# Decoder trunk with top-2 experts: sending expert outputs back to their tokens by row transfers in place of one-hot products, for seven of eight experts

## The chip, the cores and the metric

One core of a Trainium2 chip runs the whole program. The metric is the device time of one execution in microseconds (us). Times here are read either from repeated executions (the median of three) or from one profiled execution, of which the profiler kept a trace of every engine: PE is TensorE (matrix products), PEld its weight loads, DVE is VectorE, ACT is ScalarE, POOL is GpSimd, SP is SyncE, which issues most of the transfers.

## The reference

Two layers over 256 tokens of width 1024, in float32. Layer 0 mixes tokens with an mLSTM and then runs a dense feed-forward block; layer 1 mixes with an S5 recurrence and then runs the experts. Each half ends in a residual and a layer norm. The change touches the expert half of layer 1 alone:

```python
def moe_ffn(u, w_router, w13, w2):          # 8 experts, D = 1024, D_FF = 2816
    t = u.reshape(-1, D)
    logits = (t @ w_router).astype(jnp.float32)
    top_val, top_idx = lax.top_k(logits, TOP_K)      # TOP_K = 2
    top_w = jax.nn.softmax(top_val, axis=-1)
    out = jnp.zeros_like(t)
    for e in range(N_EXPERTS):
        gate_e = jnp.sum(jnp.where(top_idx == e, top_w, 0.0), axis=-1).astype(t.dtype)
        out = out + gate_e[:, None] * swiglu(t, w13[e], w2[e])
    return out.reshape(Bsz, S, D)
...
x = layer_norm(DEEPNORM_ALPHA * x + (1.0 + g_f) * y, ln_ffn_g[i], ln_ffn_b[i])
```

A token has two experts, so an expert needs to see about a quarter of the tokens.

## The kernel before, in words

The expert half is `experts` (called by `moe`). Its outer loop `e` runs over eight *places*; the router sorts the experts into them, so that the fuller ones come into even places. An even place has room for 96 tokens (`SA + SB` = 64 + 32 slots), an odd place for 64. If an expert overflows, a branch behind the loop runs a second pass; the loop itself does not depend on it.

Into a place: `gather` multiplies the tokens with one-hot matrices (token by slot), so that `xs[e]` holds the tokens of its slots, in columns.

Within a place, six blocks `b` of the hidden width:

- `first(e, b)` fetches four pieces of `moe_w13` (two in block 5) with `tile` (line 1424, on SP) and multiplies them with the tokens into `eg` and, in even places, `eu` (lines 1479 and 1489). ACT and DVE make the gated product `sg` from them (lines 1504 and 1508).
- `turned` transposes `sg` on PE (`eh`, line 1525) and ACT copies it into `hh` (line 1528).
- `second(e, b)` fetches two pieces of `moe_w2` (one in block 5), also with `tile`, and adds the products into `ey` (lines 1542 and 1546). It is put on the list `late`, and so written behind `first` of the block after, in block 0 of the place after for b = 5.

A place therefore takes 22 + 11 = 33 loads of 1 MB (1.0486 million bytes), 264 in all. Each goes into the least recently used of a ring of 15 buffers (`ring`), after the products that read the buffer's last content. In this text a place's loads are counted from 0 in the order of the code; with `late` counted in, the 9th load of a place (number 8) is the first `moe_w2` piece of its own block 0, and four loads of place e+1 are written ahead of the last load of place e.

Out of a place: `leave` multiplies `ey` by the condition row into `yt` (lines 1552 and 1554, DVE), slots in rows. Then

- `back(e)`, at block 4, makes the one-hot matrix slot by token: DVE compares (line 1429), PE transposes (line 1463, `pT`), ACT copies (line 1464);
- `scatter(e, tb)`, for each half `tb` of the tokens, multiplies `yt` with it on PE into `esc` (line 1563: six products with 64 contraction rows each in an even place, two in an odd place, for each half; the trace counts every float32 product twice) and DVE adds the product, times the token's weight for this expert, into the residual `x` (line 1566, two instructions of 128x512). The two halves go on `late` and `later`, among the blocks of the place after; the last place does both at once.

Behind the last place come `finish` (the layer norm) and the four output transfers.

What sets the order: each engine works its instructions off in the order of the code, as placed by a scheduler that runs when the program is built. SP and ACT transfers, together, take eight completion counters (`DMAHW0` to `DMAHW7`) in rotation; a transfer waits until the one before it on its counter has landed. POOL's transfers have counters of their own (`DMASW`).

Of the kernel before, what the change touches and what calls it, by code (L numbers as in the profile page):

```python
# [7 lines left out]
F32 = mybir.dt.float32  # L8
F32R = mybir.dt.float32r
BF16 = mybir.dt.bfloat16  # L10
I32 = mybir.dt.int32
U32 = mybir.dt.uint32
AF = mybir.ActivationFunctionType
ALU = mybir.AluOpType
PSUM = bass.MemoryType.PSUM

P = 128
D = 1024
# [5 lines left out]
NE = 8  # L24
SA, SB = 64, 32
# [10 lines left out]
class Trunk:  # L36
    def __init__(self, tc, ctx, I, out):
        self.tc, self.nc, self.I, self.out = tc, tc.nc, I, out
        self.n = 0
        self.const = ctx.enter_context(tc.tile_pool(name="const", bufs=1))  # L40
        self.wp = ctx.enter_context(tc.tile_pool(name="wp", bufs=3))
        self.pools = [({"raw": 4}, self.wp)]
        self.ps = ctx.enter_context(tc.tile_pool(name="ps", bufs=4, space=PSUM))
        self.ppools = [({"acc": 4}, self.ps)]
        self.fill, self.s4 = [], {}
        self.seq = 0
        self.rings, self.place, self.spare = [], {}, None
        self.raws = "raw"
        self.open(*self.pools[0])
# [1270 lines left out]
    def weights(self, top, hot):  # L1320

        V = self.nc.vector
        t3 = top.rearrange("p (t k) -> p t k", t=2)
        dl, e1, w0, w1 = (self.sm(2, n) for n in ("dl", "e1", "w0", "w1"))
        V.tensor_tensor(dl, t3[:, :, 1], t3[:, :, 0], ALU.subtract)
        self.exp_acc(e1, dl, [P, 2], "sm")
        V.tensor_scalar(w0, e1, 1.0, None, ALU.add)
        V.reciprocal(w0, w0)
        V.tensor_tensor(w1, w0, e1, ALU.mult)
        gate, out = self.sm(16, "gate"), self.sm(16, "gater", tag="keep")  # L1330
        for tb in range(2):
            s = slice(tb * 8, tb * 8 + 8)
            V.tensor_scalar(gate[:, s], hot[0][:, s], w0[:, tb:tb + 1], None, ALU.mult)
            V.scalar_tensor_tensor(gate[:, s], hot[1][:, s], w1[:, tb:tb + 1], gate[:, s], ALU.mult, ALU.add)
            self.ranked(out[:, s], gate[:, s])
        return out

    def moe(self, lng, lnb, uh, ul, slot, ranked, less, chosen, io, mxi, oi):
        nc = self.nc
# [6 lines left out]

        def ready():
            with self.tc.issue_after(self.gathered.ins):
                gate.append(self.weights(*chosen))
            parts = self.parted(self.s4[1, 5], P)  # L1350
            for h in range(2):
                pb = self.psum("adar", "aux")
                for q in range(2):
                    nc.tensor.matmul(pb[:, q * 256:q * 256 + 256], self.pick[:, 2 * h + q, 0:1].to_broadcast([P, P]),
                                     parts, start=True, stop=True)
                f = lambda o, i: nc.scalar.activation(o, i, AF.Copy, bias=1.0 / ALPHA, scale=1.0 / ALPHA)
                r = slice(64 * h, 64 * h + 64)
                f(g1[r, 0:512], pb[r])
                for q in range(2):
                    r = slice(64 * h + 32 * q, 64 * h + 32 * q + 32)  # L1360
                    f(g1[r, 512:768], pb[r, q * 256:q * 256 + 256])
# [44 lines left out]
    def experts(self, uh, ul, slot, oi, caps, gate, io, g1, sums, slot0=None, hooks=None):  # L1406
# [162 lines left out]

        late, later = [], []  # L1570
        xs, pTs = {}, {}

        def run_late():
            for f in [late.pop(0) for _ in range(len(late))]:
                f()

        def end(e, py):
            y = leave(e, py)
            if e == NE - 1:
                for tb in range(2):  # L1580
                    scatter(e, tb, y, True)
            else:
                late.append(lambda: scatter(e, 0, y))
                later.append(lambda: scatter(e, 1, y))
# [6 lines left out]
        for e in range(NE):  # L1591
            py = []
            for b in range(6):
                with self.tc.issue_after(self.gathered.ins) if hooks and (e, b) == (0, 0) else ExitStack():
                    sg = first(e, b)
                if hooks and (e, b) in hooks:
                    hooks[e, b]()
                run_late()
                mid()
                with self.tc.issue_after(self.ey.ins) if (0, 0) < (e, b) < (NE - 1, 5) else ExitStack():  # L1600
                    h = turned(*sg)
                if b == 1:
                    late += later
                    later = []
                if b == 0:
                    py += [self.pacc("ey") for _ in range(2 if caps[e] > SA else 1)]
                if b == 4:
                    back(e)
                late.append(lambda e=e, b=b, py=py, h=h: second(e, b, py, h))
                if b == 5:  # L1610
                    late.append(lambda e=e, py=py: end(e, py))
                if (e, b) in groups:
                    gather(*groups[e, b], slot)
# [5 lines left out]
    def run(self):  # L1619
        self.constants()  # L1620
        with self.phase("res", x=1, rs=24, ad=3, s4=6, acol=6):
# [29 lines left out]
            with self.phase("w", hi=2, raww=2):  # L1651
# [33 lines left out]
                with self.phase("s5o", psum=dict(work=4, aux="acc"), gg=1):  # L1685
                    with self.phase("s5a", u1=4, v=4, tmp=4, dec=2):
                        gg, w0 = self.s5(ut)
                    utp.__exit__(None, None, None)
                    s5p.__exit__(None, None, None)
                    moer = self.phase("moer", side="right", u3h=1, u3l=1, keep=10, oh=1, io=1, rawx=5)  # L1690
                    moer.__enter__()
                    for r in self.rings:
                        r[0] = self.mark if r[1] == "rawx" else r[0]
                    ln = self.t([P, 2, D], "ln", name="ln2")
                    lng, lnb = ln[:, 0], ln[:, 1]
                    with self.phase("s5b", row=3, lnt=2, gt=2, sig=2, yg=4, sm=16, w64=2, b1=3, gs=1, wr=1):
                        g1, a, b = (self.t([P, D], "row") for _ in range(3))

                        ln16 = self.t([16, P], "b1", name="ln16")
                        for i, n in enumerate("gb"):  # L1700
                            self.nc.gpsimd.dma_start(ln16[8 * i:8 * i + 8],
                                                     self.I[f"ln_mix_{n}"][1].rearrange("(k p) -> k p", p=P))
                        col = []

                        def rows():
                            self.ln_rows(1, "mix", lng, lnb)
                            col.append(self.next_cols(ln16, 1, 3, 4))
                            self.ada_row(1, 2, 1.0, g1)
                            self.next_rows(lng, lnb, 1, 3, 4, a, b, "lnt")
                            return g1  # L1710

                        stats = self.glu(gg, w0, rows)
                        self.norm(stats=stats)
                        args = self.moe_in(a, b, col[0])
# [96 lines left out]
```

## Time and profile before

| | us |
|---|---|
| median of three executions (lowest to highest) | 1383.53 (1382.74 to 1386.84) |
| the profiled execution | 1383.17 |
| its span in the trace | 1381.5 |
| PE busy, of the span | 1274.1 (92%) |
| DVE busy | 599.3 (43%) |
| ACT busy | 319.8 (23%) |
| moved by transfers | 405.87 MB, mean 294 GB/s |
| the expert stage, from 664 to 1358 | 694 |
| from the last `yt` (1358.36) to the end of the span | 23.1 |

How to read it: busy times overlap, so the engine with the largest share is not the bound of every stage. A stage is read from its own window: how much PE stood still in it, what the DMA share was, and what each engine waited for. The clock granted to TensorE is 1.00 where it runs at 2.4 GHz and near 0.5 where it runs at 1.2 GHz.

### The profile page before, as it was taken

The page shows a single profiled execution, that of the slowest core. Times are in us where ns is not written, and L with a number is a line of the kernel's source. Part 1 is how long each engine was busy: PE and PEld are TensorE (multiplying, and loading weights), DVE is VectorE, ACT ScalarE, POOL GpSimd, SP SyncE. Part 2 cuts the span into 40 slices and gives each one's busy share as a digit, 9 for nine tenths or more (in the row PEclk, how much of TensorE's full clock was granted, in tenths as well). Part 3 has the DMA queues.
Part 4 walks back from the last instruction along what each step waited for, and adds up shares of the span by engine and source line. Part 5 has one row for each costly group of instructions (what it writes and reads, how often), then busy time and mean ns, then how long its engine had stood idle before and what let it go on. Part 6 is the DMA issues. An engine that isn't in the chain of part 4 may idle for free.

```text
span 1381.5 us, 23105 instructions
## 1 busy us (share of the span) xinstructions
PE 1274.1 (92%) x9667; PEld 748.1 (54%) x9667; DVE 599.3 (43%) x1275; ACT 319.8 (23%) x574; POOL 32.8 (2%) x82
## 2 busy tenths in 40 slices
PE   6999999899699996598799999999999999999993
PEld 3788787598588885487444333343333433333331
DVE  4987688789978559866411101011010010100103
ACT  1553355243344423143111000010000100000001
POOL 1000001010000001100000000000000000000000
PEclk9899999999799998599799999999999999999997
DMA  9755438866145357335599999999999999999891
GB/s 384 265 215 212 186 130 327 343 226 255 62 156 200 114 193 287 150 126 213 188 360 346 367 421 420 420 385 369 421 420 420 358 377 420 420 420 410 356 375 36
DMA packets 57802, 405.87 MB, mean 294 GB/s; under 512 B 7110, under 2 KB 7234, under 8 KB 9170
## 3 DMA queue, kind: packets, MB, share of 16 engines
q1 hardware_dynamic: 56274, 400.97, 73.5%
q0 software_dynamic: 1408, 3.25, 0.8%
q8 instruction: 80, 1.31, 0.4%
q14 instruction: 40, 0.33, 0.1%
HBM read 403.15 MB, written 1.05 MB: 293 GB/s over the span
## 4 chain that ended last, share of the span: by engine, by line
PE 54%; DVE 2%; ACT 1%; issue 0%; DVEq 0%; ACTq 0%
PE eg L1479 24%; PE ey L1542 11%; PE eu L1489 7%; PE glu L1174 4%; PE ey L1546 3%; PE esc L1563 3%; PE gat L1445 1%; PE eh L1525 1%; PE glu L1169 0%; DVE raw L136 0%; PE pT L1463 0%; ACT uT L1234 0%; DVE yt L1552 0%; DVE x L1566 0%; DVE raw L1388 0%
## 5 line engine op out<-in xcount | busy, mean ns | idle before, releaser
L1479 PE MATMUL eg<-raw,xb 128*64 128x512 f32 (+1 forms) x960 | 206.9, 564 | 0.0
L136 DVE TENSOR_TENSOR raw<-raw,hi 128x1024 fp32r<-128x1024 f32 x130 | 157.0, 1225 | 75.2 <-ACT hi L135 74.9
L1542 PE MATMUL ey<-raw,hh 128*64 128x512 f32 x704 | 164.3, 595 | 0.0
L135 ACT CAST hi<-raw 128x1024 fp32r<-128x1024 f32 x130 | 130.8, 1047 | 133.4 <-PE f L656 46.6
L1508 DVE TENSOR_TENSOR sg<-sg,eg 128x256 f32<-128x256 f32 (+1 forms) x48 | 19.2, 399 | 259.4 <-ACT sg L1504 259.4
L1479 PEld LDWEIGHTS eg<-raw,xb 128*64 128x64 f32 x960 | 63.8, 136 | 110.8 <-issue 103.1
L1542 PEld LDWEIGHTS ey<-raw,hh 128*64 128x64 f32 x704 | 49.6, 137 | 95.2 <-issue 92.8
L656 PE MATMUL f<-uh,hi 128*128 128x256 f32 x352 | 88.6, 290 | 0.8 <-ACT uf L383 0.7
L656 PE MATMUL f<-ul,hi 128*128 128x256 f32 x352 | 87.9, 289 | 0.0
L1508 DVE TENSOR_TENSOR sg<-sg,eu 128x128 f32<-128x128 f32 (+1 forms) x24 | 6.9, 287 | 184.7 <-ACT sg L1504 184.7
L1479 PE MATMUL eg<-raw,xc 128*64 128x512 f32 (+1 forms) x384 | 83.5, 565 | 0.0
L656 PEld LDWEIGHTS f<-uh,hi 128*128 128x128 f32 x352 | 69.5, 198 | 2.0 <-ACT uf L383 1.1
L656 PEld LDWEIGHTS f<-ul,hi 128*128 128x128 f32 x352 | 69.5, 198 | 0.4
L1504 ACT ACTIVATE sg<-eg 128x256 f32<-128x256 f32 (+1 forms) x48 | 17.5, 365 | 221.4 <-PE eg L1479 221.4
L656 PE MATMUL win<-uh,hi 128*128 128x256 f32 x256 | 66.0, 295 | 1.8 <-ACT uh L363 1.5
L1528 ACT COPY hh<-eh 128x384 f32<-128x384 f32 (+3 forms) x48 | 19.3, 403 | 202.4 <-PE eh L1525 202.4
L1566 DVE SCALAR_TENSOR_TENSOR x<-esc,gater,x 128x512 f32<-128x512 f32 x32 | 23.2, 748 | 98.2 <-PE esc L1563 98.2
L656 PE MATMUL win<-ul,hi 128*128 128x256 f32 x256 | 64.8, 290 | 1.0 <-DVE ul L365 1.0
L656 PE MATMUL f<-uh,raw 128*128 128x256 f32 x352 | 47.0, 288 | 10.4 <-DVE raw L136 10.4
L656 PEld LDWEIGHTS win<-uh,hi 128*128 128x128 f32 x256 | 50.1, 196 | 8.8 <-issue 5.6
L290 DVE SCALAR_TENSOR_TENSOR aacc<-raw,ccol,aacc 128x1024 f32<-128x1024 f32 x40 | 51.1, 1278 | 3.5 <-DMA aacc<-in_ada_b_dram 2.3
L656 PEld LDWEIGHTS win<-ul,hi 128*128 128x128 f32 x256 | 50.1, 196 | 3.1 <-issue 1.7
(485 smaller groups left out, 1870.7 us busy)
## 6 DMA issues: line engine op xcount, KB each, us to landing
raw<-in_moe_w_dram SPq DMA_DIRECT2D x264, 1024.0 KB, 11.2
raw<-in_ada_w_dram SPq DMA_DIRECT2D x48, 1024.0 KB, 5.5
raw<-in_ffn_w_dram SPq DMA_DIRECT2D x33, 1024.0 KB, 4.9
raw<-in_mlstm_w_in_dram SPq DMA_DIRECT2D x16, 1024.0 KB, 6.4
raw<-in_mlstm_w_out_dram SPq DMA_DIRECT2D x8, 1024.0 KB, 6.8
raw<-in_s_w_glu_dram SPq DMA_DIRECT2D x8, 1024.0 KB, 10.5
xT<-in_xT_dram SPq DMA_DIRECT2D x1, 1024.0 KB, 17.0
x<-in_x_dram SPq DMA_DIRECT2D x1, 1024.0 KB, 9.4
```

The lines of the kernel that those rows point to most:

```text
L135: self.last_hi = self.nc.scalar.copy(hi, src)
L136: self.last_lo = self.nc.vector.tensor_sub(lo, src, hi.bitcast(F32))
L290: nc.vector.scalar_tensor_tensor(acc, raw[:, k], self.ccol[:, 2 * kk + k:2 * kk + k + 1], acc, ALU.mult, ALU.add)
L656: nc.tensor.matmul(o, w[:, k, c2 * P:(c2 + 1) * P], u[:, k], start=(w is hi and c2 == 0 and k == 0 and u is uh), stop=(w is lo and c2 == 1 ...
L1174: mm = nc.tensor.matmul(o, g[:, k, s], wt[:, k], start=False, stop=(wt is w[vg][1] and k == 7))
L1479: nc.tensor.matmul(pa[r, 0:n], x[:, k, 0:SA], w[:, kk, h * n:(h + 1) * n], start=(k == 0), stop=(k == 7))
L1489: nc.tensor.matmul(o, x[:, k, SA:SA + SB], m, start=(k == 0), stop=(k == 7))
L1508: V.tensor_tensor(sg[q, o:o + m], sg[q, o:o + m], ps[q, m:2 * m], ALU.mult)
L1542: self.ey = nc.tensor.matmul(py[0][r], hh[:, i:i + 64], ws[k // 2][:, k % 2, 512 * h:512 * h + 512], start=(b == 0 and k == 0), stop=(b == ...
L1546: self.ey = nc.tensor.matmul(py[1][r, 0:256], hh[:, c + 32 * k:c + 32 * k + 32], ws[k // 2][:, k % 2, 256 * g:256 * g + 256], start=(b == ...
L1563: nc.tensor.matmul(o, pTs[e][r, v, tb], m, start=(v == 0), stop=(v == nv - 1))
L1566: V.scalar_tensor_tensor(self.x[:, tb, sl], psc[h], gate[0][:, tb * 8 + e:tb * 8 + e + 1], self.x[:, tb, sl], ALU.mult, ALU.add, **(dict(a ...
```

## The change

For places 0 to 6 the pair `back` and `scatter` is gone. In their place:

- `store(e, y)`, at the spot where `scatter` was queued: ACT issues transfers of `yt` into a DRAM tensor `rowsd` (one row of 1024 for each slot of places 0 to 6; 576 rows). Two of 64x512 (128 KB each), and in even places four of 32x256 (32 KB each) besides: 4 even places x 6 and 3 odd places x 2 are 30 transfers, 2.36 MB.
- `returns`, called by the hook `ready` in place 0: from the router's masks and slot numbers, some 33 small DVE instructions and one on POOL make for each token two row numbers (`ri`) and two weights (`wk`; zero where the token's expert is in the last place, or where the slot overflows).
- `fetch`, in block 1 of place 7: takes two buffers out of the ring of 15 and issues on POOL four indirect transfers, each of which reads for 128 tokens the row of 1024 that `ri` names: 4 x 128 x 4 KB are 2.10 MB.
- `give`, written in block 4 of place 7: four DVE instructions of 128x1024 that add the rows, times `wk`, to `x`.

Place 7 keeps `back` and `scatter` as they were. The second pass for overflow keeps them too.

```diff
+        self.drows = ctx.enter_context(tc.tile_pool(name="drows", bufs=1, space=bass.MemoryType.DRAM))
...
-                gate.append(self.weights(*chosen))
+                g, w = self.weights(*chosen)
+                gate.append(g)
+                gate.append(self.returns(chosen[1], ranked, less, w))
...
+        def store(e, y):
+            r0 = sum(caps[:e])
+            for h, r in halves:
+                nc.scalar.dma_start(rowsd[r0:r0 + SA, 512 * h:512 * h + 512], y[r, 0:512])
+            if caps[e] > SA:
+                for g, r in quarters:
+                    nc.scalar.dma_start(rowsd[r0 + SA:r0 + SA + SB, 256 * g:256 * g + 256], y[r, 512:768])
+
+        def fetch():
+            ri = gate[1][0]
+            got.extend(self.ring("raw", [P, 2, D]) for _ in range(2))
+            for tb in range(2):
+                for k in range(2):
+                    nc.gpsimd.indirect_dma_start(got[k][:, tb], None, rowsd[:, :],
+                                                 bass.IndirectOffsetOnAxis(ap=ri[:, 2 * tb + k:2 * tb + k + 1].bitcast(U32),
+                                                                           axis=0))
+
+        def give():
+            wk = gate[1][1]
+            for tb in range(2):
+                for k in range(2):
+                    V.scalar_tensor_tensor(self.x[:, tb], got[k][:, tb], wk[:, 2 * tb + k:2 * tb + k + 1], self.x[:, tb],
+                                           ALU.mult, ALU.add)
...
         def end(e, py):
             y = leave(e, py)
-            if e == NE - 1:
+            if e < NE - 1 and hooks:
+                store(e, y)
+            elif e == NE - 1:
...
-                if b == 4:
+                if b == 4 and (not hooks or e == NE - 1):
                     back(e)
+                if hooks and (e, b) == (NE - 1, 1):
+                    fetch()
+                if hooks and (e, b) == (NE - 1, 4):
+                    give()
```

Three places in the order, all around the end of place 6, show what moves. Left out between the rows on SP are instructions without a transfer that read the expert's number.

SP before, at the end of place 6: the last `moe_w2` piece of place 6, the four `moe_w13` pieces of place 7's block 1, and the two `moe_w2` pieces of its block 0 (loads 4 to 9 of place 7).

```order
L1424 DMA raw_10249<-in_moe_w_dram 128x2048 [waits DMAHW0_49,PE_49]
L1424 DMA raw_10274<-in_moe_w_dram 128x2048 [waits DMAHW1_49,PE_49]
L1424 DMA raw_10276<-in_moe_w_dram 128x2048 [waits DMAHW2_49,PE_49]
L1424 DMA raw_10286<-in_moe_w_dram 128x2048 [waits DMAHW3_49,PE_49]
L1424 DMA raw_10288<-in_moe_w_dram 128x2048 [waits DMAHW4_49,PE_49]
L1424 DMA raw_10310<-in_moe_w_dram 128x2048 [waits DMAHW5_49,PE_49]
L1424 DMA raw_10313<-in_moe_w_dram 128x2048 [waits DMAHW6_49,PE_49]
```

Here the counters (the first number behind `DMAHW`) follow one another without a gap, each load taking the next.

SP now, the same stretch and one load more; lines are shifted by 29.

```order
L1453 DMA raw_10144<-in_moe_w_dram 128x2048 [waits DMAHW0_49,PE_49]
L1453 DMA raw_10175<-in_moe_w_dram 128x2048 [waits DMAHW1_49,PE_49]
L1453 DMA raw_10177<-in_moe_w_dram 128x2048 [waits DMAHW2_49,PE_49]
L1453 DMA raw_10187<-in_moe_w_dram 128x2048 [waits DMAHW6_49,PE_49]
L1453 DMA raw_10189<-in_moe_w_dram 128x2048 [waits DMAHW2_49,PE_49]
L1453 DMA raw_10201<-in_moe_w_dram 128x2048 [waits DMAHW3_49,PE_49]
L1453 DMA raw_10204<-in_moe_w_dram 128x2048 [waits DMAHW4_49,PE_49]
L1453 DMA raw_10226<-in_moe_w_dram 128x2048 [waits DMAHW5_49,PE_49]
```

The rotation is no longer SP's own: six counters between these loads have gone to ACT, and the loads `raw_10201` (number 8 of place 7) and those behind it wait on the counters 3, 4, 5 that ACT's stores of place 6 have taken before them.

ACT before, from the gated product of place 7's block 0 on:

```order
L1504 ACTIVATE sg_10247<-eg_10212 128x256 [waits DVE_49,PE_49]
L1528 COPY hh_10270<-eh_10267 128x256 [waits PE_49,Activation_49]
L1504 ACTIVATE sg_10298<-eg_10273 128x256 [waits DVE_49,PE_49]
L1528 COPY hh_10326<-eh_10323 128x256 [waits PE_49,Activation_49]
L1504 ACTIVATE sg_10353<-eg_10328 128x256 [waits DVE_49,PE_49]
```

ACT now, from the same instruction; `yt_10159` is the output of place 6.

```order
L1533 ACTIVATE sg_10142<-eg_10107 128x256 [waits DVE_49,PE_49]
L1612 DMA rowsd<-yt_10159 64x512 [waits DMAHW3_49,DVE_49]
L1612 DMA rowsd<-yt_10159 64x512 [waits DMAHW4_49]
L1615 DMA rowsd<-yt_10159 32x256 [waits DMAHW5_49,DVE_49]
L1615 DMA rowsd<-yt_10159 32x256 [waits DMAHW7_49]
L1615 DMA rowsd<-yt_10159 32x256 [waits DMAHW0_49]
L1615 DMA rowsd<-yt_10159 32x256 [waits DMAHW1_49]
L1557 COPY hh_10171<-eh_10168 128x256 [waits PE_49,Activation_49]
L1533 ACTIVATE sg_10199<-eg_10174 128x256 [waits PE_49]
```

Six stores of `yt` stand between the first gated product and the first copy of `hh` of place 7; the first and the third of them wait for DVE.

DVE before, from the output of place 6 on (`gater` holds the tokens' weights):

```order
L1552 TENSOR_TENSOR yt_10264<-ey_9718,g_1046_6701 128x512 [waits PE_49]
L1554 TENSOR_TENSOR yt_10264<-ey_9719,g_1046_6701 128x256 [waits PE_49]
L1566 SCALAR_TENSOR_TENSOR x_179_1172<-esc_10300,gater_7278,x_179_1172 128x512 [waits PE_49]
L1566 SCALAR_TENSOR_TENSOR x_179_1172<-esc_10301,gater_7278,x_179_1172 128x512 [waits PE_49]
L1508 TENSOR_TENSOR sg_10298<-sg_10298,eg_10273 128x256 [waits Activation_49]
L1566 SCALAR_TENSOR_TENSOR x_179_1172<-esc_10355,gater_7278,x_179_1172 128x512 [waits PE_49]
L1566 SCALAR_TENSOR_TENSOR x_179_1172<-esc_10356,gater_7278,x_179_1172 128x512 [waits PE_49]
L1508 TENSOR_TENSOR sg_10353<-sg_10353,eg_10328 128x256 [waits Activation_49]
```

DVE now, from the same instruction; `raw_10219` and `raw_10220` are the buffers into which POOL fetches rows.

```order
L1581 TENSOR_TENSOR yt_10159<-ey_9641,g_1046_6703 128x512 [waits DMAHW1_49,DMAHW0_49,PE_49]
L1583 TENSOR_TENSOR yt_10159<-ey_9642,g_1046_6703 128x256 [waits PE_49]
L1632 SCALAR_TENSOR_TENSOR x_179_1174<-raw_10219,wk_7295,x_179_1174 128x1024 [waits DMASW7_49]
L1632 SCALAR_TENSOR_TENSOR x_179_1174<-raw_10220,wk_7295,x_179_1174 128x1024 [waits DMASW0_49,DVE_49]
L1632 SCALAR_TENSOR_TENSOR x_179_1174<-raw_10219,wk_7295,x_179_1174 128x1024 [waits DMASW1_49]
L1537 TENSOR_TENSOR sg_10199<-sg_10199,eg_10174 128x256 [waits Activation_49]
L1632 SCALAR_TENSOR_TENSOR x_179_1174<-raw_10220,wk_7295,x_179_1174 128x1024 [waits DMASW2_49,DVE_49]
L1537 TENSOR_TENSOR sg_10250<-sg_10250,eg_10225 128x256 [waits Activation_49]
```

Four additions into `x` behind the output of place 6 have become four that wait for POOL's transfers (`DMASW`), and three of them stand ahead of the gated product `sg_10199` of place 7's block 1.

## Rows read from the trace of the kernel before

**Rows 1.** Windows of the expert stage, columns as the first row names them.
```profile
core 0: us, PE busy (x) PEld busy (x) DVE busy (x) ACT busy (x) POOL busy (x), PEclk, DMA share, GB/s
664.00:1358.00 694.00, 691.75 (x4748) 262.90 (x4748) 74.56 (x197) 56.70 (x159) 0.00 (x0) 0.99 0.94 382
849.00:951.00 102.00, 101.53 (x788) 39.78 (x788) 9.59 (x26) 8.37 (x24) 0.00 (x0) 1.00 0.97 391
951.00:1023.00 72.00, 72.00 (x402) 24.89 (x400) 7.59 (x16) 4.87 (x14) 0.00 (x0) 1.00 1.01 421
1297.00:1358.00 61.00, 60.30 (x298) 20.79 (x289) 5.70 (x11) 4.21 (x12) 0.00 (x0) 1.00 0.77 318
```

**Rows 2.** Waits from 660 to 1381: total us, times, longest us.
```profile
PEld eg L1479 <- DMA raw<-in_moe_w_dram: 3.8, 10, 0.8
SPq L1424 <- PE eg L1479: 180.5, 105, 3.9
SPq L1424 <- DMA raw<-in_moe_w_dram: 90.4, 54, 2.0
```

**Rows 3.** Line 1424, the weight loads: time from issue to landing.
```profile
DMA to landing us min/median/max: 4.8/11.2/19.8
```

**Rows 4.** Timeline of VectorE (start, us), line 1552, places 2, 3, 6, 7.
```profile
951.24 0.69 DVE L1552 TENSOR_TENSOR yt<-ey,g 128x512 f32<-128x512 f32 x1 [0.88 <-PE ey L1542]
1022.70 0.69 DVE L1552 TENSOR_TENSOR yt<-ey,g 128x512 f32<-128x512 f32 x1 [0.88 <-PE ey L1542]
1296.70 0.69 DVE L1552 TENSOR_TENSOR yt<-ey,g 128x512 f32<-128x512 f32 x1 [0.88 <-PE ey L1542]
1358.36 0.69 DVE L1552 TENSOR_TENSOR yt<-ey,g 128x512 f32<-128x512 f32 x1 [5.73 <-PE ey L1542]
```

**Rows 5.** Windows for line 1563 alone, the one-hot products on TensorE.
```profile
core 0: us, PE busy (x) PEld busy (x), PEclk, DMA share, GB/s
664.00:1358.00 694.00, 35.87 (x120) 12.50 (x120) 0.99 0.94 382
779.00:849.00 70.00, 3.99 (x24) 2.15 (x24) 1.00 1.01 421
849.00:951.00 102.00, 4.49 (x8) 1.18 (x8) 1.00 0.97 391
```

**Rows 6.** Windows for line 1463 alone (the transposes of the one-hot matrices).
```profile
664.00:1358.00 694.00, 5.68 (x32) 3.68 (x32) 0.99 0.94 382
849.00:951.00 102.00, 1.04 (x6) 0.67 (x6) 1.00 0.97 391
```

**Rows 7.** Timeline of SyncE, windows 838:853, 926:951.9, 1269:1297.4, 1269:1334.
```profile
838.36 12.77 SPq L1424 DMA_DIRECT2D raw<-in_moe_w_dram  x6
926.71 23.14 SPq L1424 DMA_DIRECT2D raw<-in_moe_w_dram  x10
1269.47 25.84 SPq L1424 DMA_DIRECT2D raw<-in_moe_w_dram  x10
1269.47 61.01 SPq L1424 DMA_DIRECT2D raw<-in_moe_w_dram  x25
```

**Rows 8.** DMA issues: KB each, median us from issue to landing.
```profile
out_dram<-raw SPq DMA_DIRECT2D x4, 256.0 KB, 3.7
raw<-in_ln_ffn_g_dram SPq DMA_DIRECT2D x1, 512.0 KB, 12.2
row<-in_ln_ffn_g_dram POOLq DMA_DIRECT2D x1, 512.0 KB, 4.0
```

**Rows 9.** Timeline of TensorE in place 7, its second block.
```profile
1309.11 3.60 PE L1542 MATMUL ey<-raw,hh 128*64 128x512 f32 x16
1312.64 0.44 PE L1525 MATMUL eh<-ident,sg 128*128 128x128 f32 x2
```

**Rows 10.** Windows ahead of the expert stage, columns as in rows 1.
```profile
10.00:20.00 10.00, 8.19 (x67) 2.64 (x60) 0.22 (x1) 0.37 (x1) 0.00 (x0) 1.00 1.02 425
270.00:280.00 10.00, 6.93 (x29) 5.94 (x30) 9.40 (x17) 7.93 (x13) 0.00 (x0) 0.52 0.97 378
```

More of the change, by code (lines that the diff above doesn't have):

```diff
@@ L1335, in weights, with returns @@
             self.ranked(out[:, s], gate[:, s])
-        return out
+        return out, (w0, w1)
+    def returns(self, hot, pos, less, w):
+        nc = self.nc
+        V = nc.vector
+        at = self.sm(8, "at")
+        nc.gpsimd.iota(at, [[2 * SA + SB, 4], [SA + SB, 2]], base=-1, channel_multiplier=0, allow_small_or_imprecise_dtypes=True)
+        rf, wk, ri = self.sm(4, "rf"), self.sm(4, "wk", tag="keep"), self.sm(4, "ri", dt=I32, tag="keep")
+        for tb in range(2):
+            s = slice(tb * 8, tb * 8 + 8)
+            p, ok = self.sm(8, "p"), self.sm(8, "ok")
+            V.tensor_tensor(p, pos[:, s], at, ALU.add)
+            V.tensor_scalar(ok, less[:, s], 0.0, None, ALU.is_le)
+            nc.gpsimd.memset(ok[:, NE - 1:NE], 0.0)
+            for k in range(2):
+                i = 2 * tb + k
+                h = self.sm(8, "h")
+                self.ranked(h, hot[k][:, s])
+                V.tensor_tensor(h, h, ok, ALU.mult)
+                V.tensor_reduce(wk[:, i:i + 1], h, mybir.AxisListType.X, ALU.add)
+                V.tensor_tensor(wk[:, i:i + 1], wk[:, i:i + 1], w[k][:, tb:tb + 1], ALU.mult)
+                V.tensor_tensor(h, h, p, ALU.mult)
+                V.tensor_reduce(rf[:, i:i + 1], h, mybir.AxisListType.X, ALU.add)
+        V.tensor_copy(ri, rf)
+        return ri, wk
     def moe(self, lng, lnb, uh, ul, slot, ranked, less, chosen, io, mxi, oi):
@@ L1571, in experts @@
         xs, pTs = {}, {}
+        if hooks:
+            rowsd = self.drows.tile([sum(CAPS[:-1]), D], F32, name="rowsd")
         def run_late():
@@ L1575, in run_late @@
                 f()
+        def store(e, y):
[5 more added lines that the diff above has]
+                    nc.scalar.dma_start(rowsd[r0 + SA:r0 + SA + SB, 256 * g:256 * g + 256], y[r, 512:768])
+        got = []
+        def fetch():
[8 more added lines that the diff above has]
+            wk = gate[1][1]
+            for tb in range(2):
+                for k in range(2):
+                    V.scalar_tensor_tensor(self.x[:, tb], got[k][:, tb], wk[:, 2 * tb + k:2 * tb + k + 1], self.x[:, tb],
+                                           ALU.mult, ALU.add)
         def end(e, py):
             y = leave(e, py)
-            if e == NE - 1:
+            if e < NE - 1 and hooks:
+                store(e, y)
+            elif e == NE - 1:
                 for tb in range(2):
@@ L1689, in run @@
                     s5p.__exit__(None, None, None)
-                    moer = self.phase("moer", side="right", u3h=1, u3l=1, keep=10, oh=1, io=1, rawx=5)
+                    moer = self.phase("moer", side="right", u3h=1, u3l=1, keep=12, oh=1, io=1, rawx=5)
                     moer.__enter__()
```

## The prediction

> **What bounds the kernel now.** I read the windows of the expert stage first [rows 1]. From 664 to 1358 PE is busy for 691.75 of 694 us, at a granted clock of 0.99; DVE is busy for 74.56, ACT for 56.70, POOL not at all. The reader is to see in the other three windows of the group what the average hides. An even place (849 to 951) keeps PE for 101.5 us, more than its loads take; an odd place (951 to 1023) keeps PE for all of 72.0 us while the transfers run at a share of 1.01 and 421 GB/s. At that rate a load of 1.0486 MB takes 2.49 us, and 33 of them 82.2 us, more than the 72 that the place lasts. Odd places live on a lead: loads that were fetched while the even place ahead was slow. In pairs, two places need 66 x 2.49 = 164.3 us of transfer and take 102 + 72 = 174 us of PE.
>
> The waits come next [rows 2]. PE waited for a load 10 times for 3.8 us together, at most 0.8. SP waited for buffers that PE had yet to free for 180.5 us, and for a transfer's landing for 90.4 us, 54 times. The last is the rule of the eight counters at work: a load isn't issued until the eighth before it has landed, and the longest time from issue to landing, 19.8 us [rows 3], is 8 x 2.49 = 19.9. So PE bounds every place, with a lead of loads that an odd place uses up. The times of `yt` [rows 4] are the marks that I count between: place 2 ends at 951.24, place 3 at 1022.70 (71.46 us), place 6 at 1296.70, place 7 at 1358.36 (61.66 us).
>
> **What is removed.** All one-hot products of the stage go: 35.87 us of PE [rows 5] (those of place 7 stand behind 1358), and the transposes but for place 7's two: 5.68 in all, 1.04 for an even place, so (5.68 - 4 x 1.04) / 4 = 0.38 for an odd place [rows 6], hence 5.30. Together 41.2 us. But it is worth its face value only where PE sets the pace. The products of place 0 fall in place 1 (3.99 us), those of an odd place in the even place behind it (4.49) [rows 5]; the transposes fall in their own place. So the removal is worth 1.04 up to the end of place 0, 3.99 + 0.38 = 4.37 in place 1, and 4.49 + 1.04 = 5.53 in each of places 2, 4 and 6, which PE bounds: **-22.0 us**. The remaining 19 lie in places 3, 5 and 7; the next part says why they are lost. The 15 copies of line 1464 and 28 additions into `x` that go free ACT and DVE, which are idle most of the stage [rows 1]; I count nothing for that.
>
> **What the stores do.** Their 30 transfers are 2.36 MB, 5.6 us at 421 GB/s, spread over the stage, and ACT has the time to issue them. Their price lies in the order: they take counters of the rotation that SP's loads use. A store waits for `yt`; the load that comes next on its counter waits for the store to land. So a load that before ran far ahead of PE is now tied to the end of the place before it. The order shows which: after place 6, load 8 of place 7 (`raw_10201`). In the code the stores of places 2 and 4 stand at the same spot and hold load 8 of the place behind them.
>
> What that load did before is in SP's timeline [rows 7]. Load 8 of place 3 was issued at 926.71, and ten loads from it on were out before `yt` of place 2 came at 951.24. Load 8 of place 7 was issued at 1269.47, and again ten were out before 1296.70; from it to the last there are 25. Now the ten are held: at `yt` only loads 0 to 7 are there, of which PE has already used four. The lead is lost, and the odd place runs at the speed of its loads. (Stores of odd places are two transfers and hold load 12 of the even place behind. For place 2 that one was issued at 838.36, with five more in the 12.77 us from there [rows 7]; now it comes 4.4 us behind `yt` of place 1, but an even place needs 102 / 33 = 3.1 us for a load, and eight loads are still ahead of it, some 25 us of work. Place 0's store holds load 17 of place 1, further off still. I take both at nothing; if that cover were gone, each would cost a load alone, 4.8 us.)
>
> I work out the interval from `yt` of place 2 to `yt` of place 3. First `yt` itself, 0.69 us [rows 4]. Then the store has to land: no row shows a store of `yt`; the nearest are the output transfers of 256 KB from the same kind of buffer, 3.7 us from issue to landing, and above them a load of 512 KB that shared the queue, 12.2, beside its like on POOL's queue, 4.0 [rows 8]. I take 3.7, since the queue is empty by then; the ends are 2.3 (a load of 1 MB lands in 4.8 at the least [rows 3], less its own 2.49) and 12.2. Then load 8 alone, 4.8 us. Then 28 loads at 2.49 (24 of this place and four of the next, which are written ahead of the last one), 69.7 us. Then the products on the last load, half of 3.60 [rows 9], 1.8. Sum 0.69 + 3.7 + 4.8 + 69.7 + 1.8 = 80.7 against 71.46: **+9.2**, and the same for place 5. With 1.8 us of PE for each load against 2.49, PE cannot get behind its loads there, so the 41.2 us lose their 19.
>
> The Trainium skill, "DMA: Bandwidth & Descriptors", section "Anatomy of one DMA — SWDGE (gpsimd) path", fits about 2.0 us plus bytes over 436 GB/s to one transfer, though for GpSimd's queue; by it a store of 128 KB would take 2.3 us, an estimate at the lower of my two ends, and the sum would be about 4 us lower. No run here shows a store of that size.
>
> **Fetch and give.** Place 7 ends with no next place: 24 loads behind load 8, 59.8 us. In it fall the four fetches, 2.10 MB or 5.0 us at 421 GB/s, on the same transfer engines, which are now the bound; before they were busy for 0.77 of place 7 [rows 1]. So 0.69 + 3.7 + 4.8 + 59.8 + 5.0 + 1.8 = 75.8 against 61.66: **+14.1**. No row shows an indirect transfer; its bytes could cost nothing, if the fetches fill a gap while the load 8 is held, or twice their share. The ring has 13 buffers instead of 15 from there on, which takes nothing from a place that waits for loads. The four additions of 128x1024 are twice the size of a `yt` each, some 1.4 us, on a DVE that is busy for 5.70 of 61 us. `returns` adds 33 small instructions to DVE in place 0, hidden by PE. Behind the last `yt` nothing changes.
>
> **Sum.** -22.0 + 9.2 + 9.2 + 14.1 = +10.5 against the profiled execution, 1383.17, which lies 0.4 under the median: 1393.7, forecast **1394**.
>
> **Rivals.**
>
> *Faster: loads are not held, because the store is issued and landed before its counter is next wanted.* Then the lead survives, and the stage is bound pair by pair by what is larger: transfers, 164.3 + 1.6 of stores (two sevenths of 5.6) = 165.9 against 174, -8.1 for each of three pairs, and -5.4 in places 0 and 1: -29.7, **1354**. For it: PE is the bound by rows 1, and the removed work is real. Against it: rows 3 show that the counters bind (19.8), and the order shows the same counters on ACT and SP. The rule in "DMA: Bandwidth & Descriptors", section "Issuing engines are not separate DMA queues", speaks for this rival: transfers started by the scalar, sync or gpsimd engine run on the same 16 engines and interleave, so a store would cost its bytes and nothing in order. The 90.4 us of rows 2 are time that this sentence leaves out.
>
> *No change: holding costs less than I count.* A store lands in 2.3 us (-4.2 for three places) and the fetches fill a gap (-5.0): **1385**.
>
> *Slower by DVE.* Three additions that wait for the fetches now stand on DVE ahead of the gated product of place 7's block 1. PE wants its transpose after the second pair of loads: it stood at 1312.64, 15.9 us behind `yt` [rows 9]; held, load 9 ends 0.69 + 3.7 + 4.8 + 2.49 + 1.8 = 13.5 us behind it. From there PE, at 1.8 a load, can make up 0.69 us on each of the 24 loads behind load 8, 16.6 in all. So fetches that land up to 30 us behind `yt` of place 6 cost nothing, and each us beyond costs one. At 12.2 us for each of the four, one by one behind the store, it would be 0.69 + 3.7 + 48.8 = 53: +23, **1417**. Against it: 4.0 us for 512 KB on POOL's queue [rows 8], which makes 20.
>
> *Slower by the clock.* In odd places PE will be busy for 1.8 in 2.49, 72%. The windows ahead of the stage show 8.19 us busy in 10 at a granted clock of 1.00, but 6.93 in 10 at 0.52 [rows 10], which is the lower level, 1.2 GHz. At that level a load costs PE 3.6 us, so PE would be the bound and never idle again until the clock came back. A spell of ten us in each of three places costs 3 x 10 x (1 - 2.49 / 3.6), 9 us: **1403**.
>
> **How the numbers follow.** Chances: my forecast, with store and fetch prices within their ends, 0.70; faster 0.11; no change 0.08; slower by DVE 0.05; slower by the clock 0.06. The forecast's own range goes from 1388 to 1408: stores at 2.3 and half of the fetch's bytes hidden (-6), or stores at 7 us (halfway to 12.2) at three places (+10) and fetches at double (+5). With no change and the clock in, I give **1386 to 1408**, which leaves out the faster rival, the slower by DVE and a few odd ends. A difference of 0.3%, 4.2 us, is about what a measurement can tell from none. The faster rival gives 0.11 for faster; half of "no change", with a part of the lowest forecasts, 0.09 for same; 0.80 for slower.
>
> **What would show it.** Right: lines 1563 and 1463 shrink to place 7's; the intervals between `yt` are near 81, 81 and 76 for places 3, 5 and 7, and some 5.5 shorter than before for 2, 4, 6; PE waits for loads some 40 to 60 us instead of 3.8; SP waits for a transfer into `rowsd`; the DMA share falls in the last 20 us of places 2, 4 and 6 and is near 1 through the places behind them. Wrong: place 3 still takes under 72 us, or load 8 is issued ahead of `yt`; then the hold is not there. If place 7's wait ends in DVE and not in a load, the fetches are the late ones. A clock near 0.5 in an odd place would be the last rival.

## The result and the profile after

The changed kernel takes 1393.32 us (median of four, 1392.75 to 1394.38) against 1383.64 for the kernel before, a ratio of 1.0067 with an interval of 1.0049 to 1.0084: slower by about 10 us. The forecast was 1394, the range 1386 to 1408. The profiled execution has a span of 1392.7 us.

These are the windows of the expert stage of the changed kernel, to be laid beside [rows 1] (us, busy time and instructions of each engine, granted clock, DMA share, GB/s):

```profile
core 0: us, PE busy (x) PEld busy (x) DVE busy (x) ACT busy (x) POOL busy (x), PEclk, DMA share, GB/s
664.00:1369.00 705.00, 660.99 (x4591) 243.07 (x4590) 57.57 (x189) 52.20 (x144) 4.10 (x6) 0.98 0.94 382
928.00:938.00 10.00, 10.00 (x62) 3.38 (x58) 0.42 (x1) 0.70 (x2) 0.00 (x0) 1.00 0.20 84
938.00:1021.00 83.00, 71.31 (x375) 21.88 (x374) 4.04 (x10) 4.59 (x13) 0.00 (x0) 0.98 0.98 400
1021.00:1116.00 95.00, 94.79 (x776) 37.31 (x774) 5.57 (x16) 7.45 (x21) 0.00 (x0) 1.00 0.94 388
1292.00:1369.00 77.00, 58.11 (x277) 19.25 (x277) 8.13 (x11) 4.21 (x12) 3.90 (x4) 0.89 0.95 387
1310.00:1320.00 10.00, 0.00 (x0) 0.00 (x0) 3.76 (x3) 0.00 (x0) 0.00 (x0) 0.50 1.02 418
```

PE is busy for 31 us less than in [rows 1], and the stage is 11 us longer. Place 4 (1021 to 1116) is still full; place 3 (938 to 1021) has 12 us in which PE stands. The second row tells why: in the last 10 us of place 2 the transfers run at a share of 0.20, while PE is fully busy. From load 8 of place 3 on, nothing is fetched ahead.

The outputs of the places, on DVE in the changed kernel (start, us), for places 2, 3, 4, 5, 6 and 7; compare [rows 4]:

```profile
938.05 0.69 DVE L1581 TENSOR_TENSOR yt<-ey,g 128x512 f32<-128x512 f32 x1 [0.88 <-PE ey L1571]
1020.76 0.69 DVE L1581 TENSOR_TENSOR yt<-ey,g 128x512 f32<-128x512 f32 x1 [0.88 <-DMA raw<-in_moe_w_dram]
1116.27 0.69 DVE L1581 TENSOR_TENSOR yt<-ey,g 128x512 f32<-128x512 f32 x1 [0.88 <-PE ey L1571]
1198.75 0.69 DVE L1581 TENSOR_TENSOR yt<-ey,g 128x512 f32<-128x512 f32 x1 [0.88 <-PE ey L1571]
1292.04 0.69 DVE L1581 TENSOR_TENSOR yt<-ey,g 128x512 f32<-128x512 f32 x1 [0.88 <-PE ey L1571]
1369.50 0.69 DVE L1581 TENSOR_TENSOR yt<-ey,g 128x512 f32<-128x512 f32 x1 [6.97 <-PE ey L1571]
```

From mark to mark this gives 82.71 us for place 3 and 82.48 for place 5 (71.46 before), 77.46 for place 7 (61.66 before), and 95.51 for place 4 (102.72 before).

The waits of the changed kernel from 660 to the end (total us, times, longest us), PE's and DVE's first, then SP's; compare [rows 2]:

```profile
PEld eg L1508 <- DMA raw<-in_moe_w_dram: 36.3, 35, 2.9
DVE x L1632 <- DMA raw<-rowsd,ri: 25.0, 4, 17.8
PEld ey L1571 <- DMA raw<-in_moe_w_dram: 17.5, 13, 1.5
PE eh L1554 <- DVE sg L1537: 15.8, 2, 15.1
PE eg L1508 <- DMA raw<-in_moe_w_dram: 15.4, 29, 2.1
PE ey L1571 <- DMA raw<-in_moe_w_dram: 11.6, 22, 0.7
```

```profile
SPq L1453 <- DMA raw<-in_moe_w_dram: 378.8, 162, 14.9
SPq L1453 <- DMA rowsd<-yt: 69.2, 16, 14.8
SPq L1453 <- PE eg L1508: 29.9, 23, 3.2
```

SP, which waited most for buffers that PE had yet to free (180.5 us on this line before, 29.9 now), waits for transfers to land, and 16 times for the landing of a store, a transfer that ACT has issued. PE's weight loads wait 53.8 us for transfers in two groups, and its products 27.0 us (the two overlap in time). Before the change the weight loads waited 7.0 us: the 3.8 of the one group in [rows 2], which is all that the prediction counts, 1.7 for `ey` and 1.5 for `eu`. The products had no such wait.

The hold itself, in SP's timeline of the changed kernel, windows 1118:1126 and 1294:1301:

```profile
1119.35 6.79 SPq L1453 DMA_DIRECT2D raw<-in_moe_w_dram  x9
1295.27 3.26 SPq L1453 DMA_DIRECT2D raw<-in_moe_w_dram  x5
```

Load 8 of place 5 goes out 3.08 us behind `yt` of place 4 (1116.27), load 8 of place 7 goes out 3.23 us behind `yt` of place 6 (1292.04). In [rows 7] the latter had gone out 27 us ahead of `yt`.

### The profile page after: what moved, and what is told of

Same layout as the page of the kernel before. It is cut to its first block, busy times and chain, and to the rows that moved or that the text cites. A ratio compares the mean times of both kernels' runs of the same rounds, so it can differ in the third digit from the quotient of the medians.

```text
span 1392.7 us, 22869 instructions
## 1 busy us (share of the span) xinstructions
PE 1243.3 (89%) x9517; PEld 729.0 (52%) x9517; DVE 582.0 (42%) x1270; ACT 315.5 (23%) x559; POOL 38.4 (3%) x89
## 3 DMA queue, kind: packets, MB, share of 16 engines
q10 hardware_dynamic: 1888, 2.36, 0.6%
## 4 chain that ended last, share of the span: by engine, by line
PE 41%; DMA 14%; DVE 2%; ACT 1%; issue 0%; ACTq 0%; SPq 0%; DVEq 0%
PE eg L1508 17%; DMA raw<-in_moe_w_dram 13%; PE ey L1571 7%; PE eu L1518 6%; PE glu L1175 3%; PE ey L1575 3%; PE gat L1474 1%; PE eh L1554 1%; PE glu L1170 0%; DMA rowsd<-yt 0%; DVE raw L137 0%; ACT uT L1235 0%; DVE x L1595 0%; DVE raw L1420 0%; DVE raw L1417 0%
## 5 line engine op out<-in xcount | busy, mean ns | idle before, releaser
L1571 PE MATMUL ey<-raw,hh 128*64 128x512 f32 x704 | 165.5, 598 | 12.3 <-DMA raw<-in_moe_w_dram 11.6
L1508 PEld LDWEIGHTS eg<-raw,xc 128*64 128x64 f32 x384 | 24.4, 136 | 53.1 <-issue 33.2
```

The lines of the kernel that those rows point to most:

```text
L1508: nc.tensor.matmul(pa[r, 0:n], x[:, k, 0:SA], w[:, kk, h * n:(h + 1) * n], start=(k == 0), stop=(k == 7))
L1571: self.ey = nc.tensor.matmul(py[0][r], hh[:, i:i + 64], ws[k // 2][:, k % 2, 512 * h:512 * h + 512], start=(b == 0 and k == 0), stop=(b == ...
```

## The experiments

The theory is that of the prediction: stores on ACT take counters that SP's loads need next, hold those loads until the output of an even place is stored, and so take away the lead on which the odd place behind it lives. The rivals: the bytes of stores and fetches slow the loads; the wait of DVE for the fetches costs the time; the removal itself does it. In each diff the lines stand against the changed kernel, unless it says otherwise.

**Stores from another queue.**

```diff
         def store(e, y):
...
-                nc.scalar.dma_start(rowsd[r0:r0 + SA, 512 * h:512 * h + 512], y[r, 0:512])
+                nc.gpsimd.dma_start(rowsd[r0:r0 + SA, 512 * h:512 * h + 512], y[r, 0:512])
...
-                    nc.scalar.dma_start(rowsd[r0 + SA:r0 + SA + SB, 256 * g:256 * g + 256], y[r, 512:768])
+                    nc.gpsimd.dma_start(rowsd[r0 + SA:r0 + SA + SB, 256 * g:256 * g + 256], y[r, 512:768])
```

> The changed kernel with one edit: the 30 stores are issued by GpSimd, whose transfers have counters of their own, so that no weight load shares a counter with a store. Same bytes, same fetches. Theory (held loads): places 3 and 5 get their lead back; places 2+3 and 4+5 together come to about 166 us instead of 178.3 and 178.0, and the kernel to 1360 to 1370, the rest of the gain being eaten in place 7, where PE waits some 15 us or more for the fetches that stand ahead on DVE (the lead no longer hides that wait). Rival (bytes: stores and fetches slow the weight loads by their traffic): nothing changes, 1390 to 1395. Rival (wait for the fetches on DVE is what costs): nothing changes in places 2 to 5, 1390 to 1395.

Measured 1369.49, ratio to before 0.9885 (0.9863 to 0.9908). The marks are 67.66 us apart for place 3 and 71.81 for place 5, hence 163.2 for places 2+3 and 167.3 for 4+5; place 7 takes 74.30. So some 24 us of the changed kernel's time hang on the engine that issues the stores, at the same bytes. In this kernel's windows the last 10 us of place 2 show full transfers, where the changed kernel had 0.20, and place 7 shows PE idle at the lower clock:

```profile
928.00:938.00 10.00, 10.00 (x72) 3.61 (x70) 0.00 (x0) 0.32 (x1) 0.00 (x0) 1.00 1.02 423
...
1280.00:1290.00 10.00, 0.50 (x4) 0.00 (x0) 0.69 (x1) 0.00 (x0) 3.90 (x4) 0.72 1.01 417
1290.00:1300.00 10.00, 1.49 (x4) 0.58 (x6) 3.49 (x4) 0.37 (x1) 0.00 (x0) 0.50 1.03 421
```

PE's timeline in this kernel names what it waited for there, the gated product that stands on DVE behind three additions of fetched rows:

```profile
1298.51 0.69 PE L1554 MATMUL eh<-ident,sg 128*128 128x128 f32 x2 [18.01 <-DVE sg L1537]
```

**The same queue, another place.** The stores of places 0, 2 and 4 stay on ACT, but are put behind the last copy of `hh` of the place after.

```diff
...
-            if e < NE - 1 and hooks:
+            if e in (0, 2, 4) and hooks:
+                due[e + 1, 5] = lambda: store(e, y)
+            elif e < NE - 1 and hooks:
                 store(e, y)
...
                     h = turned(*sg)
+                if (e, b) in due:
+                    with self.tc.issue_after(self.turn.ins):
+                        due.pop((e, b))()
```

(`self.turn` is the copy of line 1557.)

> The changed kernel with the stores of places 0, 2 and 4 put off on ACT until the last block of the place behind; they stay on ACT and on the shared counters, and the store of place 6 stays where it was. Theory (held loads): the loads that are held now stand at the end of an odd place, where the lead is used up anyway and an even place follows; places 2+3 and 4+5 fall to about 166 us each (from 178.3 and 178.0), place 7 stays near 77.5, the kernel 1366 to 1372. Rivals (bytes; wait for the fetches): unchanged, 1390 to 1395.

Measured 1374.24, ratio 0.9920 (0.9900 to 0.9940), a little above the expected 1366 to 1372. Places 2+3 take 95.55 + 70.21 = 165.8, places 4+5 95.65 + 72.96 = 168.6 instead of 166, place 7 stays at 76.77. So it is not ACT as the issuer that costs, but where in the order the store stands: SP still waits 17 times for a store to land, but 45.6 us together instead of 69.2.

Both edits leave one rival open that the prediction didn't name. With its stores, ACT itself comes late to the copy `hh` that PE needs: 22.2 us in the changed kernel, in four waits. The trace of the changed kernel settles it. First one of the four waits (start, us), then all that PE waited for in place 5, from 1116.27 to 1198.75 (total us, times, longest us):

```profile
1120.31 0.37 ACT L1557 COPY hh<-eh 128x256 f32<-128x256 f32 x1 [5.37 <-DMA rowsd<-yt]
```

```profile
PE eg L1508 <- DMA raw<-in_moe_w_dram: 7.9, 15, 1.9
PE ey L1571 <- DMA raw<-in_moe_w_dram: 4.9, 9, 0.6
```

PE stood for loads and for nothing else in place 5, and so it did in place 3 (11.6 us). While ACT was held, PE worked on the products of the next block, which ended at 1124.6; the copy ran at 1120.31.

**Only the removal.** Stores, fetches and additions are left out.

```diff
             if e < NE - 1 and hooks:
-                store(e, y)
+                pass
...
-                if hooks and (e, b) == (NE - 1, 1):
-                    fetch()
-                if hooks and (e, b) == (NE - 1, 4):
-                    give()
```

> Only the removal: the changed kernel without stores, fetches and additions (the output lacks the seven experts). Theory (held loads): no load is held, places go pair by pair at the speed of the larger of loads (164.3 us) and products; places 2+3 and 4+5 about 164 to 165, place 7 about 62 or less, the kernel 1350 to 1356. Rival (the removal itself makes odd places wait for loads, since PE is faster in the even place ahead and builds less lead): places 3 and 5 stay near 82, the kernel 1385 to 1390.

Measured 1350.81, ratio 0.9755 (0.9739 to 0.9771). Place 3 takes 65.58 and place 5 70.26; 2+3 are 161.1 and 4+5 165.8. The removal is worth 34 us when nothing holds the loads, and by itself it makes PE's products wait for loads only for 8.5 us in the whole stage (27.0 in the changed kernel), so odd places don't stay near 82. It does bring the stage to the edge of what the transfers can deliver: its windows for all of place 7 and for its first 26 us:

```profile
1264.00:1325.00 61.00, 55.78 (x277) 18.33 (x269) 2.98 (x7) 4.21 (x12) 0.00 (x0) 1.00 0.95 394
1264.00:1290.00 26.00, 26.00 (x134) 8.81 (x128) 1.85 (x4) 1.88 (x5) 0.00 (x0) 1.00 1.01 421
```

**Only the stores.** The kernel before with all its one-hot products, and the 30 stores on ACT besides.

```diff
             else:
+                if hooks:
+                    store(e, y)
                 late.append(lambda: scatter(e, 0, y))
                 later.append(lambda: scatter(e, 1, y))
```

> The kernel before with the 30 stores on ACT added; all one-hot products are kept and the stored rows are never read. Theory (held loads): the stores alone stretch places 3 and 5 to about 82 us from 71.5 and place 7 from 61.7 to about 72, even places stay at 102.7: the kernel 1412 to 1418, more than the changed one, though it moves less. Rival (a store costs its 5.6 us of bytes at most): 1384 to 1390.

Measured 1413.68, ratio 1.0221 (1.0204 to 1.0238). Place 3 takes 79.88, place 5 80.53, place 7 72.57; the even places 102.74, 102.73 and 99.82, as before. 2.36 MB of stores that nobody reads cost 30 us. Its windows, the last 13 us of place 2 and then place 3:

```profile
940.00:953.00 13.00, 13.00 (x86) 4.51 (x82) 0.42 (x1) 0.70 (x2) 0.00 (x0) 1.00 0.01 1
953.00:1033.00 80.00, 74.05 (x399) 23.86 (x397) 7.28 (x15) 4.88 (x14) 0.00 (x0) 1.00 0.97 398
```

For 13 us the transfers stand at a share of 0.01, with PE fully busy. This is what bytes cannot do.

**No fetches.** The stores stay on ACT; the two calls of `fetch` and `give` are left out, so the seven experts' outputs never reach `x`.

> The changed kernel without the four fetches and the four additions behind them (the output lacks the seven experts); the stores stay on ACT. Theory (held loads): all intervals up to place 6 as in the changed kernel, 82.7 and 82.5 us for places 3 and 5; place 7 falls from 77.5 by the 5.0 us of the fetches' bytes and not by the 15 us that PE waited there for DVE: 71 to 73, the kernel 1387 to 1389. Rival (the wait on DVE for the fetches sets the end of place 7): place 7 falls by some 15 us, the kernel to about 1378. Rival (bytes): between the two at most, with places 3 and 5 unchanged.

Measured 1390.49, ratio 1.0040 (1.0027 to 1.0052), 1.5 us above the expected range; the kernel before stood 1.0 higher in that comparison too (1384.65). The medians differ by 2.8 us from the changed kernel. In the profile places 3 and 5 take 82.14 and 82.36, as in the changed kernel, and place 7 takes 71.72, as expected, against 77.46: the fetches and their additions are worth 5.7 us in place 7, near the 5.0 of the fetches' bytes, and not the 15 us that PE waited for them.

**The additions later.** Against the changed kernel, only the place of `give`:

```diff
...
-                    V.tensor_tensor(sg[q, o:o + m], sg[q, o:o + m], ps[q, m:2 * m], ALU.mult)
+                    self.upped = V.tensor_tensor(sg[q, o:o + m], sg[q, o:o + m], ps[q, m:2 * m], ALU.mult)
...
-                if hooks and (e, b) == (NE - 1, 4):
-                    give()
+                if hooks and (e, b) == (NE - 1, 2):
+                    with self.tc.issue_after(self.upped.ins):
+                        give()
```

> The changed kernel, stores on ACT, with only the four additions moved behind the gated product of place 7's block 2. Theory (held loads bound place 7; PE's 15 us wait for the fetches is caught up, since the loads come later still): no change against the changed kernel, 1392 to 1395. Rival (the wait on DVE lengthens place 7 of the changed kernel): 1378 to 1386.

Measured 1394.79, ratio 1.0080 (1.0062 to 1.0098): no faster. PE's 15 us wait is gone, and in its place PE waits for loads; place 7 takes 76.44.

**Both edits.** Stores on GpSimd and the additions later.

> Stores on GpSimd, as in e1_pool_stores, and besides the four additions of fetched rows are queued on DVE behind the gated product of place 7's block 2, so that nothing PE waits for stands behind them until they can run. Theory: in e1_pool_stores PE waited 18 us in place 7 for the fetches and had no later wait to hide it in; without it place 7 falls from 74 to 57 to 60 us and the kernel to 1350 to 1356, near the 1350.8 of the removal alone. Rival (the fetches' bytes, not the wait, lengthen place 7): 1364 to 1369.

Measured 1361.45, ratio 0.9842 (0.9822 to 0.9862): the fastest version that computes everything, 32 us under the changed kernel and 22 under the one before. But it lies between my two ranges: place 7 fell from 74.30 to 67.94, not to 60. PE's wait is gone, and the transfers are the bound, as this kernel's windows of place 7 show:

```profile
1267.00:1280.00 13.00, 13.00 (x74) 4.42 (x74) 1.54 (x3) 1.13 (x3) 3.43 (x7) 1.00 1.01 420
1280.00:1290.00 10.00, 10.00 (x49) 3.19 (x46) 1.71 (x2) 0.38 (x2) 3.45 (x4) 1.00 1.01 418
1290.00:1300.00 10.00, 6.08 (x26) 1.57 (x26) 2.89 (x3) 0.37 (x1) 0.00 (x0) 1.00 1.02 419
1300.00:1310.00 10.00, 7.87 (x36) 2.23 (x34) 1.30 (x2) 0.76 (x2) 0.00 (x0) 1.00 1.01 415
```

My expectation took place 7 to be bound by PE once nothing is held. The run with only the removal shows that it isn't: it takes 61.39 us there with 55.78 us of PE. So each byte that is added should count: the two kernels differ by 10.0 us in their spans (1358.8 and 1348.8), and stores and fetches together are 4.46 MB, 10.6 us at 421 GB/s. That the bytes are the whole of the 10.0 is argued from this sum; no run adds the bytes alone.

## Why the prediction was right

The mechanism is the one forecast, and shown from both sides: stores alone, on a kernel that keeps its products, cost 30 us; in the changed kernel the same stores on a queue with its own counters, or at another place in the rotation, give back 24 and 19 us. The time is right to 1 us, but that is partly luck: the gain of the even places was put too small by 4.3 us in all, and the loss of places 3, 5 and 7 by 5.6.

| term | predicted, us | measured, mark to mark |
|---|---|---|
| up to the end of place 0 | -1.04 | -1.65 (777.49 against 779.14) |
| place 1 | -4.37 | -4.37 (65.00 against 69.37) |
| places 2, 4, 6 | -5.53 each | -7.17, -7.21, -6.53 |
| places 3, 5 | +9.2 each | +11.25, +11.02 (82.71 and 82.48 against 71.46) |
| place 7 | +14.1 | +15.80 |
| last `yt` | +10.5 | +11.14 (1369.50 against 1358.36) |

**The removed products** were undersized by 1 to 1.7 us in an even place. PE's groups in place 4, 1022.7 to 1125.4 before and 1020.8 to 1116.3 after (busy us, mean ns of one):

```profile
L1479 PE MATMUL eg<-raw,xc 128*64 128x512 f32 (+1 forms) x192 | 42.8, 565 | 0.0
L1542 PE MATMUL ey<-raw,hh 128*64 128x512 f32 x88 | 21.5, 597 | 0.0
L1489 PE MATMUL eu<-raw,xc 128*32 128x256 f32 x288 | 19.9, 383 | 0.0
L1563 PE MATMUL esc<-yt,pT 64*128 64x512 f32 x8 | 4.5, 641 | 0.3 <-DVE yt L1552 0.3
```

```profile
L1508 PE MATMUL eg<-raw,xc 128*64 128x512 f32 (+1 forms) x192 | 41.3, 565 | 0.0
L1571 PE MATMUL ey<-raw,hh 128*64 128x512 f32 x88 | 20.6, 597 | 0.0
L1518 PE MATMUL eu<-raw,xc 128*32 128x256 f32 x288 | 19.5, 382 | 0.0
```

The products that stay are as many and as long one by one, but the busy times of their groups together are 2.8 us less. Groups overlap at their seams, so not all of that is time gained; PE as a whole shows what is (the same two stretches, columns as in [rows 1]):

```profile
1022.70:1125.42 102.72, 102.19 (x795) 40.08 (x799) 9.30 (x22) 8.37 (x24) 0.00 (x0) 1.00 0.95 384
```

```profile
1020.76:1116.27 95.51, 95.30 (x781) 37.62 (x785) 5.81 (x16) 7.45 (x21) 0.00 (x0) 1.00 0.94 386
```

PE is busy for 6.89 us less where the removed rows were 5.53, and stands for 0.32 less (the first removed product had waited for `yt`). I had counted the removed rows alone, and a row's own busy time is not all that it takes from its neighbours: the removed products had broken the others into shorter runs. That the breaks are the cause is argued from these rows, not tested by itself.

**The held place** was undersized by 2 us, and the trace says where. Three parts of place 5, by the chain of work that ended last in the changed kernel (start, us):

```profile
1165.74 19.80 DMA raw<-in_moe_w_dram
...
1185.58 1.94 PE eg L1508 x8
1187.52 1.00 PE eu L1518 x16
...
1196.99 1.72 PE ey L1571 x8
```

From `yt` to load 8 are 3.08 us where I had 0.69 + 3.7 = 4.39, since the two stores that come first landed within 2.2 and 2.5 us of their issue, at the lower of my ends. From load 8 to the first load of place 6, the 24th behind it, the loads set the time: 66.2 us from 1119.35 to 1185.54, where I had 4.8 + 24 x 2.49 = 64.6. The loads came a little slower than 2.49 us each; the runs don't show why. Then the chain leaves the loads: the four that are written ahead belong to an even place, and PE needs both `eg` and `eu` for each. From 1185.54 to `yt` at 1198.75 are 13.2 us, all of PE, where I had four loads and 1.8 us, 11.8. So the parts were off by -1.3, +1.6 and +1.4. The last has a reason: I gave the tail the speed of the transfers, although it consists of the next place's products.

By the fit in the Trainium skill, "DMA: Bandwidth & Descriptors", section "Anatomy of one DMA — SWDGE (gpsimd) path", a store of 128 KB takes 2.3 us, an estimate. The 2.2 and 2.5 us of this trace agree, though ACT had issued the stores.

The hold also reaches further than I wrote. The six stores take six of eight counters, so that load 7 (behind place 6, load 6 too) must share what is left with a load right ahead of it; SP's longest wait for a load to land, 14.9 us, is that of load 7 of place 3.

The stores of odd places I had taken at nothing. The loads behind them went out some 7 us behind `yt` (7.3 in place 4) instead of 4.4, and that was free: places 2 and 4 take 95.56 and 95.51 us here, and 95.55 and 95.52 in the run with only the removal, which has no stores.

**Fetch and give.** The fetch was priced at 5.0, and 5.7 is what place 7 loses without it; the rest of place 7, 70.8 by my sum, is 71.72 in the run without fetches. The rival of a slow fetch came true in half: the fetches' additions ran only from 1311 on, and PE stood for 15 us. PE in place 7 of the changed kernel:

```profile
1320.48 0.69 PE L1554 MATMUL eh<-ident,sg 128*128 128x128 f32 x2 [15.07 <-DVE sg L1537]
1321.10 9.68 PE L1508 MATMUL eg<-raw,xb 128*64 128x512 f32 x32
...
1352.58 1.94 PE L1571 MATMUL ey<-raw,hh 128*64 128x512 f32 x8 [0.17 <-DMA raw<-in_moe_w_dram]
```

It resumed 28.4 us behind `yt`, inside the 30 us that the prediction gave as the point from which it costs; by 1352.58 it had caught up with the loads. The run with the additions moved shows that the wait cost about 1 us there (77.46 against 76.44 for place 7) and the whole kernel nothing. It was hidden only because loads were late anyway: in the run with stores on GpSimd the same wait was worth 6.4 of the 8 us between 1369.49 and 1361.45.

**Clock.** The rival of the clock hardly came. Places 3 and 5 ran at 0.98 and 1.00, with PE busy for 71 and 70 of 83 us. In place 3 the lower level shows once, for some 3 us, right behind a stretch in which PE was busy for about half of 5 us:

```profile
966.00:971.00 5.00, 2.76 (x13) 0.83 (x14) 0.00 (x0) 0.37 (x1) 0.00 (x0) 1.00 1.01 415
971.40:974.70 3.30, 3.30 (x10) 0.71 (x8) 0.00 (x0) 0.00 (x0) 0.00 (x0) 0.50 1.02 425
```

It cost 0.6 us at most: place 3 takes 82.14 us in the run without fetches, where its clock was 1.00 throughout. In place 7 the clock was low where PE stood for 15 us (0.50 from 1310 to 1320) and for a while behind it.

**The faster rival**, put at 1354, describes the world without the hold. The run with only the removal stands at 1350.81, and the best complete version at 1361.45. The Trainium skill, "DMA: Bandwidth & Descriptors", section "Issuing engines are not separate DMA queues", spoke for it; for bytes its rule fits what is measured here (10.0 us for 4.46 MB), for order it does not: with the stores on another engine the kernel is 24 us faster.

## What to carry to other kernels

In this kernel a transfer that waits for a result is a gate for every transfer behind it that shares its completion counter, even when another engine issues it. Before putting a store beside a stream of prefetches, look in the order which load comes next on each of its counters and how far ahead of its use that load was issued; give the store a queue with counters of its own, or put it where the stream has no lead to lose. And count the saved work only in the stages in which that engine sets the time: here 41 us of products were removed, the removal alone brought 34, and the best version with its 4.46 MB of added transfers kept all but some 11 of these.

## What the runs showed of the hardware

- A fetch of 128 rows of 4 KB kept POOL busy for about 1 us, but four of them, issued within 5 us beside the weight loads, came in one after the other: DVE's additions on them start at 1311.28, 1315.12, 1318.81 and 1322.67, about 3.8 us apart, or 138 GB/s for the 0.52 MB of each. From issue to landing they took 9.0 to 16.5 us, in the median 12.7.
- The granted clock fell to 0.50 within PE's wait of 15 us, and the 32 products behind it took 9.68 us instead of the 7.09 of the same group later in the place.
- Stores of 128 KB landed 2.2 to 2.9 us behind their issue where no load was under way as they were issued (behind places 2, 4 and 6), and 5.4 to 7.9 us behind it where loads were (behind places 0, 1, 3 and 5).
